# A four-layer decoder trunk on one core: HGRN2's levels in shared series, its outputs turned on VectorE, and norm pieces beside the next layer's work

## The chip, the cores and the metric

The kernel runs on one core of a Trainium2 chip. The metric is the time of one execution in device microseconds (us), shown as the median of three runs. The profile is of one further execution, whose own time is given beside its span.

## The reference

The reference computes four layers over 1024 tokens of width 1024, with mixers HGRN2, sliding-window attention, gated DeltaNet and HGRN2 again. Cut to what the change touches:

```
for i in range(4):
    shift, scale, gate = split(c @ ada_w[i] + ada_b[i])
    h = rmsnorm(x, norm_g[i]) * (1 + scale) + shift
    y = mixer(h)
    x = x + gate * y

# HGRN2, per head of 128, per chunk: b = cumsum(log_f)
A[t, s] = sum_d q[t, d] k[s, d] exp(b[t, d] - b[s, d])        (s <= t)
o = A @ v + (q * exp(b)) @ S
S = exp(b_last) * S + (k * exp(b_last - b)).T @ v
y = (rmsnorm(o, onorm_g) * silu(z)) @ w_out
```

## The kernel before

**Tiling.** x is held transposed (features on partitions) in two halves of 512 tokens, `x[0]` and `x[1]`, 8 blocks of 128x512 each. Every projection is a product of float32 split into a high and a low part (`hi`, `lo`), three matmuls each (`mm3`, lines 201 to 206). `load_w` (166 to 186) brings 128x512 raw weights in over SP's DMA queue into 3 buffers (`RAW`), ScalarE casts the high part (179) and VectorE subtracts for the low part (180), 4 buffers each (`WB`). `proj_fm` (509) runs a 128-column projection for one or both halves, `proj_tm` (1170) one of 256 columns with tokens on partitions.

**Norm.** `norm_stats` (469) makes the row scale and spreads it over partitions into a PSUM bank. `norm_apply` (496) then makes, for each of 8 blocks, `n_t = x * G * rb` on VectorE (504), `hhi = n_t + S` on ScalarE (505) and `hlo` on VectorE (506). `n_t` has 2 SBUF buffers. At a layer's end the main loop (1443 to 1462) runs the norm of the next layer for each half, complete, ahead of the next layer's instructions.

**Order.** The kernel is written as Python generators. `weave` (68) takes from several of them in turn, in proportion to a total given by hand for each; `early` and `tc.high_priority` raise the priority of what is inside. From program order and priority a scheduler makes one fixed order for each engine, and PE, VectorE, ScalarE and SP each run theirs in that order.

**HGRN2** (`hgrn2`, 956). Of each of 8 heads `proj` (969) makes q, f, z and derived tiles, and `mix` (1026) runs beside the next head's projections. For each half, one after the other, `mix` goes through three levels `l` = 1, 3, 5: ScalarE and VectorE fill a tile `X` (1061 to 1063, one buffer), PE makes products of 32-wide blocks into a bank `lev_ps` (16 for level 3, 32 for level 1 at line 1040, 12 for level 5 at line 1087, on 32-column strips of the array), and VectorE picks them into `A` and scales on (1070 to 1098). `tied` (138) puts the products of a series straight behind one another on PE. Then come kh transposes (1104), four chunks of output and state products (1114 to 1124), the norm of the output on VectorE (1132), four PE transposes `ot_ps` (1136), the gate with `zs` (1139) and one 256 KB write to `od` in DRAM (1141). Before the output projection `out_load` (1185) reads `od` back.

**Gated DeltaNet** (`gdn`, 537) starts with the projections of k, q and z of unit 0 for half 0 (920), spills x, runs `decays`, and so on; `conv` (636) is three VectorE steps (650) between ScalarE copies (644, 648) and a tanh (651). Its outputs already go a way without PE: a VectorE multiply in a block order (858), a 32x32 block transpose on VectorE (859) and four 64 KB writes (862). `swa` (1219) starts with k and v of half 0, then of half 1, then q and z of the first group.

```
            r = self.rsqrt(ms, NC, "hg", mp)
            on = tl("tmp")
            nc.vector.tensor_tensor(on..., po..., r..., ALU.mult)
            pt = self.psum("tr", "ot_ps", 1)
            for c in range(NC):
                nc.tensor.transpose(pt[:, cs], on[:, cs], self.ident)
            of = tl("tmp")
            nc.vector.tensor_tensor(of, pt, d["zs", hf], ALU.mult)
            nc.sync.dma_start(od[...], of)
```

## Time and profile before

| | |
|---|---|
| median of 3 runs | 2688.89 us (2688.8 to 2697.25) |
| the profiled execution, its own time | 2695.95 us |
| its span, first to last instruction | 2694.2 us (1.75 us lie around it) |
| PE, VectorE (DVE), ScalarE (ACT) busy | 2609.7, 2010.2, 1272.9 us |
| mean granted TensorE clock | 0.992 |

The layers lie at about 62 to 640 us (HGRN2), 640 to 1118 (attention), 1118 to 2080 (DeltaNet) and 2080 to 2694 (HGRN2). PE's matmuls are pipelined: a record of 0.39 us can start 0.23 us after the one before, so what a group of matmuls costs is read from the distance of starts, not from its record lengths. "Idle" in a row is what the engine waited just before those instructions, and the name behind it is what ended most of that wait.

### The profile page before, as it was taken

The numbers are of one execution on the slowest core, as the hardware profiler recorded it, in microseconds if no ns is written. First come the engines' busy times: TensorE is split into PE (matmuls) and PEld (weight loads), VectorE is DVE, ScalarE is ACT, GpSimd is POOL, SyncE is SP. The second block draws the span as 40 slices with busy tenths as digits, with TensorE's granted clock in tenths as the row PEclk, the third lists the DMA queues.
The fourth block names the chain that finished last, engine by engine and source line by source line (L and its number), as shares of the span: only waits on it lengthen the run. The fifth ranks groups of instructions, "written<-read, shape, count | busy, mean of one in ns | idle before, by whom it ended". The sixth has DMA issues, their size and how long they took to land.

```text
span 2694.2 us, 51458 instructions
## 1 busy us (share of the span) xinstructions
PE 2609.7 (97%) x18927; PEld 2102.4 (78%) x18927; DVE 2010.2 (75%) x5619; ACT 1272.9 (47%) x3268; POOL 136.7 (5%) x352
## 2 busy tenths in 40 slices
PE   8999999999999999999999999999999999999998
PEld 4878878778878777677877777777788878787877
DVE  6776766788687877777988888989876766656575
ACT  4333333444454655454556556666644433333342
POOL 0000100000000000001001101100000000000000
PEclk9999999999999999999999999999999999999999
DMA  6332222344223252333343333333584221111133
GB/s 241 92 93 84 68 79 72 110 137 157 59 87 103 75 158 91 114 98 84 102 115 99 96 105 100 94 97 82 179 254 132 71 60 37 56 51 43 49 118 115
DMA packets 361490, 273.29 MB, mean 101 GB/s; under 512 B 70499, under 2 KB 294166, under 8 KB 361238
## 3 DMA queue, kind: packets, MB, share of 16 engines
q1 hardware_dynamic: 360950, 268.96, 33.9%
q8 instruction: 149, 2.44, 0.4%
q14 instruction: 103, 0.84, 0.1%
q0 software_dynamic: 288, 1.05, 0.1%
HBM read 224.77 MB, written 45.15 MB: 100 GB/s over the span
## 4 chain that ended last, share of the span: by engine, by line
PE 71%; DVE 17%; DMA 5%; ACT 3%; issue 3%; SPq 1%; POOL 0%; DVEq 0%; ACTq 0%; POOLq 0%
PE proj_ps L206 10%; PE proj_ps L205 9%; PE proj_ps L204 9%; PE outp_ps L204 5%; PE outp_ps L205 5%; PE outp_ps L206 5%; DMA ada_w<-in_ada_w_dram 3%; PE projt_ps L204 3%; PE projt_ps L206 3%; PE projt_ps L205 3%; DVE w_lo L180 2%; DVE gd_tb L650 2%; PE pv_ps L1374 1%; DVE ada_acc L413 1%; PE w_ps L890 1%
## 5 line engine op out<-in xcount | busy, mean ns | idle before, releaser
L204 PE MATMUL proj_ps<-hhi,w_hi 128*128 128x512 f32 x1664 | 675.8, 406 | 6.1 <-ACT gd_tb L648 5.9
L206 PE MATMUL proj_ps<-hhi,w_lo 128*128 128x512 f32 x1664 | 679.9, 409 | 0.0
L205 PE MATMUL proj_ps<-hlo,w_hi 128*128 128x512 f32 x1664 | 671.2, 403 | 0.0
L204 PEld LDWEIGHTS proj_ps<-hhi,w_hi 128*128 128x128 f32 x1664 | 315.3, 190 | 59.4 <-ACT gd_tb L648 6.3
L205 PEld LDWEIGHTS proj_ps<-hlo,w_hi 128*128 128x128 f32 x1664 | 314.7, 189 | 59.0 <-issue 2.4
L206 PEld LDWEIGHTS proj_ps<-hhi,w_lo 128*128 128x128 f32 x1664 | 315.0, 189 | 56.1 <-issue 1.0
L179 ACT CAST w_hi<-w_raw 128x512 fp32r<-128x512 f32 x332 | 202.0, 611 | 303.3 <-PE proj_ps L205 188.1
L180 DVE TENSOR_TENSOR w_lo<-w_raw,w_hi 128x512 fp32r<-128x512 f32 x332 | 223.1, 674 | 155.2 <-ACT w_hi L179 129.1
L205 PE MATMUL projt_ps<-w_lo,hhi 128*128 128x256 f32 x896 | 258.7, 291 | 4.7 <-DVE w_lo L180 4.7
L204 PE MATMUL projt_ps<-w_hi,hhi 128*128 128x256 f32 x896 | 257.8, 290 | 0.6 <-ACT w_hi L179 0.6
L206 PE MATMUL projt_ps<-w_hi,hlo 128*128 128x256 f32 x896 | 256.8, 290 | 0.0
L204 PE MATMUL outp_ps<-o_hi,w_hi 128*128 128x512 f32 x576 | 229.2, 400 | 4.7 <-ACT o_hi L1200 3.4
L205 PE MATMUL outp_ps<-o_lo,w_hi 128*128 128x512 f32 x576 | 229.4, 399 | 0.0
L206 PE MATMUL outp_ps<-o_hi,w_lo 128*128 128x512 f32 x576 | 226.8, 396 | 0.7 <-DVE w_lo L183 0.7
L205 PEld LDWEIGHTS projt_ps<-w_lo,hhi 128*128 128x128 f32 x896 | 171.1, 192 | 8.1 <-DVE w_lo L180 6.0
L204 PEld LDWEIGHTS projt_ps<-w_hi,hhi 128*128 128x128 f32 x896 | 171.1, 192 | 3.7 <-ACT w_hi L179 1.0
L206 PEld LDWEIGHTS projt_ps<-w_hi,hlo 128*128 128x128 f32 x896 | 170.8, 192 | 2.4 <-issue 1.0
L650 DVE SCALAR_TENSOR_TENSOR gd_tb<-gd_xs,taps,gd_tb 128x512 f32<-128x512 f32 x192 | 145.2, 756 | 28.3 <-ACT gd_tb L648 19.7
L182 ACT ACTIVATE w_hi<-w_raw,par 128x512 fp32r<-128x512 f32 (+1 forms) x136 | 94.3, 698 | 137.0 <-PE outp_ps L205 89.2
L204 PEld LDWEIGHTS outp_ps<-o_hi,w_hi 128*128 128x128 f32 x576 | 108.8, 189 | 29.1 <-ACT o_hi L1200 4.9
L413 DVE SCALAR_TENSOR_TENSOR ada_acc<-ada_w,par,ada_acc 128x512 f32<-128x512 f32 x140 | 104.8, 749 | 33.4 <-DMA ada_w<-in_ada_w_dram 32.5
L206 PEld LDWEIGHTS outp_ps<-o_hi,w_lo 128*128 128x128 f32 x576 | 108.7, 189 | 23.5 <-DVE w_lo L183 1.3
(398 smaller groups left out, 4894.8 us busy)
## 6 DMA issues: line engine op xcount, KB each, us to landing
ada_w<-in_ada_w_dram SPq DMA_DIRECT2D x160, 256.0 KB, 2.8
w_raw<-in_hg_in_w_dram SPq DMA_DIRECT2D x136, 256.0 KB, 2.8
w_raw<-in_gd_in_w_dram SPq DMA_DIRECT2D x108, 256.0 KB, 3.0
o_in<-od SPq DMA_DIRECT2D x72, 256.0 KB, 3.2
w_raw<-in_gd_out_w_dram SPq DMA_DIRECT2D x64, 256.0 KB, 2.9
w_raw<-in_sw_in_w_dram SPq DMA_DIRECT2D x48, 256.0 KB, 2.9
w_raw<-in_hg_out_w_dram SPq DMA_DIRECT2D x40, 256.0 KB, 2.8
ada_w<-in_ada_w_dram SPq DMA_DIRECT2D x8, 1024.0 KB, 9.2
```

Of the source, the lines that this page charges most:

```text
L179: nc.scalar.copy(hi, raw)
L180: nc.vector.tensor_tensor(lo, raw, hi.bitcast(F32), ALU.subtract)
L182: nc.scalar.activation(hi, raw, AF.Copy, scale=scale)
L204: mm(out, a[0], b[0], start=start, stop=False)
L205: mm(out, a[0], b[1], start=False, stop=False)
L206: mm(out, a[1], b[0], start=False, stop=stop)
L413: self.nc.vector.scalar_tensor_tensor(acc, w, c, acc, ALU.mult, ALU.add)
L650: nc.vector.scalar_tensor_tensor(y, xs[:, j:j + HT], w(j), y, ALU.mult, ALU.add)
L890: nc.tensor.matmul(po[:, hd[a]], dd["u"][a, hf][:, cs], rhs, start=True, stop=True)
L1374: nc.tensor.matmul(po[a * 64:(a + 1) * 64], vg[:, n + 1 - nkb + b, :], p4[:, :, a, :], start=b == 0, stop=b == nkb - 1)
```

## The change

- **HGRN2 levels.** `mix` now takes level l of half 1 together with the next level of half 0: the series of products are (half 0, 1), (half 1, 1 with half 0, 3), (half 1, 3 with half 0, 5) and (half 1, 5). The products of one series are tied. The last head is still done half by half. Level 5 has 16 products instead of 12: the 96 columns of strip 0 become 32 on strip 3 and 64 on strip 0. Buffers change with it.
- **HGRN2 outputs.** For heads 0 to 6 the PE transposes go. VectorE multiplies into block order, transposes 32x32 blocks, four DMAs write to a new DRAM tile `pd`; later `gate` reads `pd` back (256 KB), multiplies by `zs` on VectorE and writes `od`.
- **Norm.** `norm_apply` becomes a generator, `n_t` moves from SBUF to the PSUM banks `lev` (2), and the pieces of half 1 are issued by the next layer: at once in HGRN2 and attention, and in DeltaNet four behind the convolution steps of each of the first two projections. DeltaNet's early part also has z of unit 1 for half 0, and the weave that follows is 10400 shorter.
- **Attention's start.** v and q of half 0 come first, then v of half 1, k of all tokens (its row scales for two blocks at a time), z, and q of half 1.
- **Output.** `x_out` has 3 buffers instead of 5; half 1 uses the 3 raw weight buffers too.

```diff
-NB = {"n_acc": 1, "n_sq": 2, "n_t": 2}
+NB = {"n_acc": 1, "n_sq": 2}
...
+                if hf and c % 2:
+                    xo = self.wp.tile([P, HT], F32, name="x_raw", tag="raw", bufs=RAW)
+                else:
+                    xo = op.tile([P, HT], F32, name="x_out", tag="x_out", bufs=3)
...
         for k in range(KT):
-            t = self.np.tile([P, HT], F32, name="n_t", tag="n_t", bufs=NB["n_t"])
+            t = self.psum("lev", "n_t", 2)
...
+            yield 1
...
             for j in (2, 1, 0):
-                nc.vector.scalar_tensor_tensor(y, xs[:, j:j + HT], w(j), y, ALU.mult, ALU.add)
+                last = nc.vector.scalar_tensor_tensor(y, xs[:, j:j + HT], w(j), y, ALU.mult, ALU.add)
+
+            with self.tc.issue_after(last.ins):
+                drain(take(self.last, self.parts))
...
-        self.early(proj_kq(0, ds[0], ((0,),)), EV)
+        self.parts = 4
+        self.early(chain(proj_kq(0, ds[0], ((0,),)), proj_z(1, ds[1], (0,))), EV)
+        drain(self.last)
...
-              (chain(proj_z(0, ds[0], (1,)), proj_v(0, ds[0]), proj_z(1, ds[1]), proj_kq(1, ds[1])), 72800, 0, 1, 0))
+              (chain(proj_z(0, ds[0], (1,)), proj_v(0, ds[0]), proj_z(1, ds[1], (1,)), proj_kq(1, ds[1])), 62400, 0, 1, 0))
...
-        bufs = {"X": 1, "q": 3, "f": 3, "kg": 3, "qf": 3, "tmp": 3, "v": 3, "zs": 3, "kht": 1, "k0": 2}
+        bufs = {"X": 2, "q": 3, "f": 2, "kg": 4, "qf": 4, "tmp": 3, "v": 3, "zs": 4, "kht": 1, "k0": 2}
...
+        def gate():
+
+            h, hf, z = pend.pop(0)
+            rows = (slice(h * P, (h + 1) * P), slice(hf * HT, (hf + 1) * HT))
+            t = tl("tmp")
+            nc.sync.dma_start(t, self.pd[rows])
+            nc.vector.tensor_tensor(v4(z, "c b"), v4(t, "b c"), v4(z, "c b"), ALU.mult)
+            nc.sync.dma_start(od[rows], z)
...
+                mms = [lambda c=c, m=m: mm(c, *m) for c in range(NC) for m in (
+                    (0, 3, slice(6, 7), slice(3, 4)), (0, 0, slice(0, 4, 3), slice(1, 3)),
+                    (1, 1, slice(1, 5, 3), slice(2, 4)), (2, 2, slice(2, 3), slice(3, 4)))]
...
+            if h < HA:
+
+
+                nc.vector.tensor_tensor(v4(on, "b c"), v4(po, "c b"), r[:, :, None, None].to_broadcast([P, NC, 4, 32]), ALU.mult)
+                ob = tl("tmp")
+                nc.vector.transpose(ob, on)
+                dst = self.pd[h * P:(h + 1) * P, hf * HT:(hf + 1) * HT].rearrange("(b q) (a t) -> a q b t", b=4, a=4)
+                for a in range(4):
+                    nc.sync.dma_start(dst[a], ob[a * 32:(a + 1) * 32].rearrange("q (b t) -> q b t", b=4))
+                pend.append((h, hf, d["zs", hf]))
...
+        def mix(h, d, halves=(0, 1)):
+
+            for hf in halves:
+                level_1(d, hf)
+            steps = [[(halves[0], 1)], [(halves[0], 3)], [(halves[0], 5)], []]
+            for hf in halves[1:]:
+                for n, l in ((1, 1), (2, 3), (3, 5)):
+                    steps[n].append((hf, l))
+            for n, st_ in enumerate(steps):
+                ls = [level(d, hf, l) for hf, l in st_]
+                if ls:
+                    self.tied([m for mms, _ in ls[::-1] for m in mms])
+                    yield 700 + 300 * len(ls)
+                if n == 1 and pend:
+                    gate()
+                for _, rest in ls:
+                    rest()
+                    yield 1
+                if n == 3 and ls:
+                    gate()
+                if n > 1 and n - 2 < len(halves):
+                    yield from outputs(h, d, halves[n - 2])
...
-        self.early(kv(0))
+        self.early(chain(proj_v(0), proj_q(0, ds[0], (0, 1))))
         self.spill_x(1)
-        drain(kv(1))
-        ds = [dict() for _ in range(G)]
-        drain(proj(0, ds[0]))
+        drain(proj_v(1))
+        drain(self.proj_tm(self.load_tm(w_in, 1024), ev_k))
+        drain(chain(proj_z(0, ds[0]), proj_q(0, ds[0], (2, 3))))
...
-                k.norm(nxt, hf)
-                if nxt % 3 and hf == 0:
-                    k.spill_x(0)
-                if hf == 1:
+                a = k.norm_apply(nxt, hf, k.norm_stats(hf))
+                if hf == 0:
+                    drain(a)
+                    if nxt % 3:
+                        k.spill_x(0)
+                else:
+                    k.last = a
                     k.nst.close()
```

## Rows read from the trace of the kernel before

**Rows 1.** The page, part 1: busy time, share of the span, instructions.

```profile
PE 2609.7 (97%) x18927; PEld 2102.4 (78%) x18927; DVE 2010.2 (75%) x5619; ACT 1272.9 (47%) x3268; POOL 136.7 (5%) x352
```

**Rows 2.** PE's waits over the span: engine line waited for: us, times, longest.

```profile
PE lev_ps L1040 <- DVE hg_X L1063: 6.8, 19, 1.8
...
PE proj_ps L204 <- ACT gd_tb L648: 5.9, 1, 5.9
PE ot_ps L1136 <- DVE hg_tmp L1132: 5.6, 11, 1.3
PE projt_ps L205 <- DVE w_lo L180: 4.7, 5, 1.4
...
PE ab_ps L575 <- DVE gd_tb L727: 2.0, 1, 2.0
```

**Rows 3.** Stretches: length, busy us (instructions) of PE, PEld, DVE, ACT, POOL; clock, DMA.

```profile
62.00:520.00 458.00, 446.93 (x4209) 370.84 (x4208) 321.64 (x1012) 162.58 (x388) 28.75 (x60) 1.00 0.28 83
...
1180.00:1260.00 80.00, 77.21 (x534) 62.41 (x535) 63.55 (x161) 40.38 (x109) 8.31 (x20) 0.96 0.39 103
2140.00:2540.00 400.00, 396.14 (x3772) 332.79 (x3771) 247.46 (x848) 143.14 (x345) 25.76 (x56) 1.00 0.16 48
```

**Rows 4.** PE's timeline around one group of output transposes: start, us, line, count.

```profile
365.37 0.39 PE L205 MATMUL proj_ps<-hlo,w_hi 128*128 128x512 f32 x1
365.59 0.60 PE L1136 MATMUL ot_ps<-ident,hg_tmp 128*128 128x128 f32 x4
...
366.26 0.39 PE L204 MATMUL proj_ps<-hhi,w_hi 128*128 128x512 f32 x1
```

**Rows 5.** PE's timeline around series of levels 1, 3 and 5 of one head.

```profile
2225.94 0.55 PE L1040 MATMUL lev_ps<-hg_X,hg_kg 128*32 128x48 f32 x32
2226.31 0.52 PE L1040 MATMUL lev_ps<-hg_q,hg_k 128*32 128x48 f32 x32
...
2228.71 0.39 PE L206 MATMUL proj_ps<-hhi,w_lo 128*128 128x512 f32 x1
2229.07 0.55 PE L1040 MATMUL lev_ps<-hg_X,hg_kg 128*32 128x48 f32 x32
2229.55 0.50 PE L204 MATMUL proj_ps<-hhi,w_hi 128*128 128x512 f32 x1
2229.89 0.39 PE L205 MATMUL proj_ps<-hlo,w_hi 128*128 128x512 f32 x1
...
2232.40 0.39 PE L204 MATMUL proj_ps<-hhi,w_hi 128*128 128x512 f32 x1
2232.72 0.85 PE L1087 MATMUL lev_ps<-hg_X,hg_kg 128*32 128x96 f32 x24
2233.50 0.50 PE L205 MATMUL proj_ps<-hlo,w_hi 128*128 128x512 f32 x1
```

**Rows 6.** VectorE's groups: count, busy us, mean ns, idle before.

```profile
L506 DVE SCALAR_TENSOR_TENSOR hlo<-n_t,mod,hhi 128x512 fp32r<-128x512 f32 x64 | 45.9, 746 | 1.4 <-ACT hhi L505 0.8
...
L859 DVE STREAM_TRANSPOSE gd_of<-gd_of 128x512 f32<-128x512 f32 x32 | 22.5, 704 | 0.1
...
L1198 DVE TENSOR_TENSOR o_z<-o_in,o_z 128x512 f32<-128x512 f32 x32 | 21.8, 687 | 9.6 <-DMA o_z<-zd 6.6 <-issue 1.4 <-DMA o_in<-od 1.2
```

**Rows 7.** ScalarE's groups, 2140 to 2540 us: count, busy us, mean ns, idle before.

```profile
L179 ACT CAST w_hi<-w_raw 128x512 fp32r<-128x512 f32 x58 | 36.1, 622 | 72.0 <-PE proj_ps L205 52.2 <-PE projt_ps L206 11.2 <-DMA w_raw<-in_hg_in_w_dram 7.0
...
L1090 ACT COPY hg_at<-lev_ps 32x384 f32<-32x384 f32 (+2 forms) x42 | 15.2, 363 | 20.3 <-PE lev_ps L1087 19.6
```

**Rows 8.** DMA issues over the span: count, KB each, median us to landing.

```profile
o_in<-od SPq DMA_DIRECT2D x72, 256.0 KB, 3.2
...
od<-gd_of SPq DMA_DIRECT2D x128, 64.0 KB, 1.8
```

**Rows 9.** One stretch at DeltaNet's start, columns as in rows 3.

```profile
1134.50:1141.00 6.50, 3.69 (x9) 2.82 (x9) 5.77 (x10) 4.07 (x8) 2.74 (x9) 0.50 0.33 80
```

**Rows 10.** SP's timeline in DeltaNet: four output writes together, start and us.

```profile
1547.70 1.77 SPq L862 DMA_DIRECT2D od<-gd_of  x4
```

More of the change, by code (lines that the diff above doesn't have):

```diff
@@ L100, in __init__ @@
         self.x = [None, None]
-        self.oo, self.pre = {}, {}
+        self.oo, self.pre, self.last, self.parts = {}, {}, iter(()), 0
     def hslot(self, name):
@@ new lines, in outputs @@
+        def outputs(h, d, hf):
+            kg, qf, v, at, F, S = d["kg", hf], d["qf", hf], d["v", hf], ats[hf], d["F", hf], d.get("S")
+            pt = self.psum("tr", "kh_ps", 1)
+            for c in range(NC):
+                cs = slice(c * P, (c + 1) * P)
+                nc.tensor.transpose(pt[:, cs], kg[:, cs], self.ident)
+            yield 436
+            kht = tl("kht")
+            nc.scalar.copy(kht, pt)
+            po = self.psum("o", "o_ps", 1)
+            ssq = mp.tile([P, NC], F32, name="hg_ssq", tag="hg_ssq", bufs=2)
+            on = tl("tmp")
+            for c in range(NC):
+                cs = slice(c * P, (c + 1) * P)
+                if S is not None:
+                    nc.tensor.matmul(po[:, cs], qf[:, cs], S, start=True, stop=False)
+                nc.tensor.matmul(po[:, cs], at[:, c, :], v[:, c, :], start=S is None, stop=True)
+                yield 436
+                if not (hf == 1 and c == NC - 1):
+                    pS = self.psum("s", "s_ps", 1)
+                    nc.tensor.matmul(pS[:, :P], kht[:, cs], v[:, c, :], start=True, stop=True)
+                    Sn = mp.tile([P, P], F32, name="hg_S", tag="hg_S", bufs=3)
+                    if S is None:
+                        nc.vector.tensor_copy(Sn, pS[:, :P])
+                    else:
+                        nc.vector.scalar_tensor_tensor(Sn, S, F[:, c:c + 1], pS[:, :P], ALU.mult, ALU.add)
+                    S = Sn
+                    yield 218
+                nc.scalar.activation(on[:, cs], po[:, cs], AF.Square, accum_out=ssq[:, c:c + 1])
+            ms = mp.tile([P, NC], F32, name="hg_ms", tag="hg_ms", bufs=2)
+            nc.vector.tensor_scalar(ms, ssq, 1.0 / P, EPS, ALU.mult, ALU.add)
+            r = self.rsqrt(ms, NC, "hg", mp)
+            if h < HA:
[6 more added lines that the diff above has]
+                pend.append((h, hf, d["zs", hf]))
+            else:
@@ L1278, in ev_k @@
[L1278 to L1286 removed]
+            if tp % 2 == 0:
+                ks["ms"] = sp.tile([P, 16], F32, name="k_ms", tag="k_ms", bufs=1)
@@ L1291, in ev_v, with proj_q @@
             nc.scalar.copy(v[:, v2, :], p3)
[L1293 to L1294 removed]
+        def proj_q(g, d, tps=range(4)):
             def ev_q(tp, ps):
@@ L1434, in trunk @@
                 k.preload(hg_in_w[0], (x,))
-        k.norm_apply(layers[0], 0, rb)
-        rb = k.norm_stats(1, k.load_x(sp, 1))
-        k.norm_apply(layers[0], 1, rb)
+        drain(k.norm_apply(layers[0], 0, rb))
+        k.last = k.norm_apply(layers[0], 1, k.norm_stats(1, k.load_x(sp, 1)))
+        drain(k.last)
         if layers[0] % 3:
```

228 lines of the change are left out of this document (96 added, 132 removed).

## The prediction

> **What bounds the kernel now.** I read the busy times first. PE is busy for 97% of the span, VectorE for 75% and ScalarE for 47% [rows 1], so a gain has to come out of PE's own work or out of its waits. PE's waits come second. They are short and scattered, and the reader should note the names: matmuls that wait for VectorE's X tile, one wait of 5.9 us behind a ScalarE convolution copy, eleven in front of the output transposes, five for the low weights [rows 2]. Third come the stretches. In the two HGRN2 layers PE is busy 446.93 of 458 us and 396.14 of 400, VectorE 321.64 and 247.46, ScalarE 162.58 and 143.14 [rows 3], so added VectorE and ScalarE work has cover there. Last comes PE's timeline, where the distance between starts gives a price. Between 2229.89 and 2232.40 us lie eleven steps of ordinary projection matmuls, 0.228 us each [rows 5]; what a foreign group adds is the distance between the projection matmuls around it, less these steps.
>
> The sum below is made against the profiled execution, 2695.95 us; the median is 7.06 us lower, 2688.89, and I subtract the same sum from it. A measurement of this kernel can tell about 0.3%, 8 us, from no change.
>
> **Output transposes.** Four PE transposes go for each of 2 layers x 7 heads x 2 halves, 28 groups. One group stretches the distance of its neighbours from 365.37 to 366.26 us; less two steps of 0.228 it costs 0.43 us [rows 4]. 28 x 0.43 = 12.2 us. The 5.6 us that PE waited ahead of them [rows 2] fall on 32 groups, so 28/32 go, 4.9 us. Together -17.1; it is at least -12.2, if another VectorE step of the chain is waited for instead. What takes their place is off PE: a block transpose on VectorE of 704 ns [rows 6], 28 x 0.70 = 19.7 us over both layers, beside some 290 us in which VectorE is idle in the two stretches [rows 3]; the multiplies before and behind it stay, at the 687 ns that DeltaNet's gate takes in the same block order [rows 6].
>
> **SP's queue** gets four writes instead of one, a read and a write for each group; four such writes take 1.77 us of issue [rows 10]. The final write to `od` stands behind the read's landing (3.2 us for a like read [rows 8]) and a multiply of 0.69: about 3.9 us in which weight loads queue behind it. The cover is that weights are early. The casts that open a weight buffer wait 63.4 us for PE to free one and 7.0 for a DMA [rows 7]. Three raw buffers hold 3 x 24 matmuls x 0.228 = 16 us of PE's work. VectorE's gate waits for its read too: in DeltaNet the same step waits 9.6 us in 32 [rows 6], 0.3 each. I put 28 x 0.15 = +4 us on PE, between 0 and 28 x 0.7 = +20.
>
> **Level 5.** Its products run on strips of 32 columns side by side. A series of level 3 puts 4 x 48 = 192 columns on each strip and takes 0.48 us from its first start to the next projection; level 5 puts 4 x 96 = 384 on the fullest strip and takes 0.78 [rows 5]. So 192 columns cost 0.30. With the fullest strip at 256 it should take 0.48 + 0.10 = 0.58, and 32 series x 0.20 = -6.4 us. The other end is 0: if products and not columns set the pace, 16 instead of 12 give nothing back. I take -6.4, because 16 products of level 3 do run in 0.48. The Trainium skill (TensorEngine Tiling (Array Packing), section Instruction Overhead) says that each matmul has some 60 cycles of overhead on trn2, so that short ones cost as much as 60 columns; by that the rebalanced series would gain nothing, and the sum would be 6.4 us smaller, 2656 for the median, inside the forecast's own range. The trace speaks against it here: 32 records of 48 columns start within 0.37 us, 12 ns apart [rows 5]. ScalarE copies four blocks instead of three, 32 x 0.36 = 12 us more [rows 7], hidden by the 64% of these stretches in which it is idle [rows 3].
>
> **Series in common.** A lone series of level 3 adds 2229.89 - 2228.71 - 2 x 0.228 = 0.72 us to PE. A second sixteen products inside a series adds 0.37 [rows 5]. So each join saves 0.35; 14 heads x 2 joins give -9.8 us. The other end is 0: the cost of entry and exit could come back if products of one series wait for each other. I take -9.8, as the series is tied and the half whose X is made last goes first. The 6.8 us of waits for X [rows 2] I leave as they are: fewer series wait, but each for the later of two tiles. Between -4 and +8 is open.
>
> **Norm beside DeltaNet's start.** Now ScalarE reaches the first convolution copy only behind the norm's pieces, and PE waits 5.9 and then 2.0 us [rows 2]. Across the end of the first wait the clock is at half, 1.2 GHz, for 6.5 us with 3.69 us of PE work [rows 9], which costs 1.85. All of this, 9.7 us, goes if the convolution is issued first and 48 more matmuls of half 0 (z of unit 1, 11 us) stand ready. But they come out of the cover of the inverse that follows, where PE already has 2.8 us idle in 80 and VectorE works 63.6 of 80 [rows 3]. The split projection also loads its weights twice: 4 more loads, casts and subtractions, beside work. I take -8, between -9.7 and +3.
>
> **Attention's start.** PE waits 4.7 us for low weights that VectorE makes too late, between norm pieces and k's evaluation [rows 2]. With v and q first and k later, I take -3; the ends are -4.7 and, as q's evaluation asks as much of VectorE as k's, 0.
>
> **Small parts.** k's row scales for two blocks at once, the PSUM home of `n_t` (same operations, same sizes) and HGRN2's buffer counts cost nothing on PE; each lies beside projections, and a shortage would show as a wait of an evacuation. Fewer `x_out` buffers in the first half: +1, between 0 and +5.
>
> **Sum.** -17.1 + 4 - 6.4 - 9.8 - 8 - 3 + 1 = -39.3 us. That gives 2656.6 for a profiled execution and 2649.6 for the median; 2650.
>
> **Rivals.**
> *The levels wait (2670).* VectorE becomes the pace where two halves' levels come at once. PE's longest wait for X today is 1.8 us [rows 2]; if each of the 28 joined series waits 0.7 us more, 20 us come back. For it: VectorE's 70% is an average over a head. Against: the work is the same, spread over the same head.
> *The norm pieces and the levels get in each other's way (2670).* `n_t` now shares its two PSUM banks with attention's scores at the end of that layer, eight pieces of three 0.75 us steps [rows 6] over two banks, 9 us; and neither start brings anything: 39.3 - 11 - 9 = 19.3. Against: most of that chain has output projections beside it.
> *SP's queue holds up the weights (2700, slower).* At each of the 28 gates the queue stands for 3.9 us behind the read. If the loads behind it are needed at once, PE loses half of that, 28 x 1.95 = 55 us, in place of the 4: -39.3 - 4 + 55 = +11.4. It decides once the weights' lead falls below those 3.9 us; the casts' 7.0 us for DMA against 63.4 for PE [rows 7] speak against it.
> *The change doesn't join the series (2660).* The scheduler could leave them apart; then the 9.8 us stay. Against: they are tied explicitly.
>
> **How the numbers follow.** Forecast 0.56 (own range 2630 to 2662), waiting levels 0.15, norm in the way 0.12, no joins 0.06, SP's queue 0.07, and 0.04 for a gain beyond 2626, all terms at their best ends. The range 2626 to 2676 takes in the unknown bounds and the cases down to the waiting levels, and leaves out SP's queue and some of either tail. Faster by over 0.3% means below 2680.8: the forecast and nearly all of the three weaker cases, 0.87. Within 0.3%, where two of them fall together: 0.06. Slower: 0.07.
>
> **What would show it.** Right: `ot_ps` falls from 32 groups to 4; the level-5 series takes about 0.58 us; four level series a head instead of six, 28 fewer; no wait near 5.9 us at DeltaNet's start and no stretch at 0.50 there; HGRN2's two layers shorter by some 16 us each. Wrong: casts that wait for weight DMAs by more than some 7 us a layer; waits of `lev_ps` for X well over 7 us; new waits of scores for `n_t`; a VectorE above 85% in HGRN2.

## The result, and the profile after

The changed kernel takes 2696.12 us (median of 22 runs, 2690.86 to 2703.11) against 2691.15 for the kernel before (22 runs on the same chips). The ratio is 1.0020, 95% interval 1.0013 to 1.0026: 0.2% slower, within the 0.3% that the forecast called no change. The forecast was 2650, faster by 39.3 us. The profiled execution after took 2696.45 us, its span 2694.8.

The page's part 1 answers to [rows 1]:

```profile
PE 2590.9 (96%) x19071; PEld 2092.7 (78%) x19071; DVE 2025.7 (75%) x5629; ACT 1275.6 (47%) x3304; POOL 135.7 (5%) x352
```

PE's work did shrink, by 18.8 us. The span did not. So PE's idle time grew by as much: span less busy was 84.5 us and is 103.9. PE's waits say where; they answer to [rows 2]:

```profile
PE lev_ps L1079 <- DVE hg_X L1071: 8.5, 17, 2.0
PE proj_ps L207 <- DVE w_lo L181: 6.3, 2, 4.1
PE lev_ps L1079 <- DVE hg_F L1112: 4.4, 10, 0.6
...
PE outp_ps L207 <- DVE w_lo L184: 3.9, 2, 3.2
...
PE lev_ps L1079 <- DVE rs_y L164: 3.7, 2, 2.1
...
PE projt_ps L206 <- DVE w_lo L181: 2.3, 4, 1.2
```

The level series, which waited 6.8 us for X, now wait 8.5 + 4.4 + 3.7 us in the rows shown, though a head has four of them and not six. Two waits of DeltaNet's start, 5.9 us for a convolution and 2.0 for the gates, are gone; two for low weights, 6.3 us, are there. The wait of 3.2 us in the row of `outp_ps` is new too: it stands at the end of layer 0, where the kernel before waits 0.7 for low weights. The 4.7 us at attention's start are 2.3. The 5.6 us ahead of the output transposes are gone with the transposes: one group of 16 is left, 4 for each of four halves.

```profile
L1170 PE MATMUL ot_ps<-ident,hg_tmp 128*128 128x128 f32 x16 | 2.5, 280 | 0.2 <-DVE hg_tmp L1166 0.2
```

The same stretches as in [rows 3], same columns:

```profile
62.00:520.00 458.00, 438.42 (x4193) 367.74 (x4192) 330.10 (x1030) 165.30 (x405) 25.18 (x60) 0.99 0.33 99
1180.00:1260.00 80.00, 76.81 (x367) 62.30 (x366) 66.17 (x174) 43.09 (x117) 2.62 (x12) 1.00 0.38 110
2140.00:2540.00 400.00, 390.37 (x3870) 330.54 (x3869) 260.64 (x868) 144.75 (x362) 28.34 (x56) 1.00 0.21 64
```

VectorE is busy 72% and 65% of the HGRN2 stretches, not over 85%: by the average there is room. One step of a head, between the starts of two joined series, looks otherwise. PE's timeline, then the same 5.6 us as a stretch:

```profile
2338.72 0.54 PE L1079 MATMUL lev_ps<-hg_X,hg_kg 128*32 128x48 f32 x31 [0.37 <-DVE hg_X L1071]
...
2339.88 0.50 PE L206 MATMUL proj_ps<-hlo,w_hi 128*128 128x512 f32 x1
...
2343.46 0.39 PE L206 MATMUL proj_ps<-hlo,w_hi 128*128 128x512 f32 x1
2344.32 0.54 PE L1079 MATMUL lev_ps<-hg_X,hg_kg 128*32 128x48 f32 x31 [0.47 <-DVE hg_F L1112]
```

```profile
2338.70:2344.30 5.60, 5.12 (x112) 4.05 (x113) 5.60 (x25) 1.71 (x4) 1.97 (x4) 1.00 0.16 50
```

VectorE works 5.60 of 5.60 us; PE has sixteen projection products to fill the time (2339.88 to 2343.46), and then waits 0.47. So a wait here is VectorE's time from one series to the next, less what PE was given to do meanwhile. Both can be at fault, and the experiments had to tell which.

In these stretches SP's queue and ScalarE's casts are not it. The casts wait 7.8 us for weight DMAs in the last stretch, 7.0 before [rows 7], and the gates wait 14.4 us in 28, 0.5 each, where 0.3 had been taken from DeltaNet:

```profile
L180 ACT CAST w_hi<-w_raw 128x512 fp32r<-128x512 f32 x58 | 36.1, 622 | 64.0 <-PE proj_ps L206 50.1 <-DMA w_raw<-in_hg_in_w_dram 7.8 <-PE projt_ps L207 4.2
```

VectorE's groups over the span, as in [rows 6]:

```profile
L1160 DVE STREAM_TRANSPOSE hg_tmp<-hg_tmp 128x512 f32<-128x512 f32 x28 | 19.8, 706 | 0.3
L1044 DVE TENSOR_TENSOR hg_zs<-hg_tmp,hg_zs 128x512 f32<-128x512 f32 x28 | 19.3, 689 | 14.4 <-DMA hg_tmp<-pd 14.1
```

### The profile page after: what moved, and what is told of

It is laid out like the page before. It is cut to its first block, busy times and chain, and to the rows that moved or that the text cites. A ratio compares the mean times of both kernels' runs of the same rounds, so it can differ in the third digit from the quotient of the medians.

```text
span 2694.8 us, 51993 instructions
## 1 busy us (share of the span) xinstructions
PE 2590.9 (96%) x19071; PEld 2092.7 (78%) x19071; DVE 2025.7 (75%) x5629; ACT 1275.6 (47%) x3304; POOL 135.7 (5%) x352
## 4 chain that ended last, share of the span: by engine, by line
PE 40%; DVE 11%; DMA 2%; issue 1%; ACT 1%; SPq 1%; POOL 0%; DVEq 0%; ACTq 0%
PE proj_ps L207 6%; PE proj_ps L206 6%; PE proj_ps L205 6%; PE outp_ps L206 3%; PE outp_ps L205 3%; PE outp_ps L207 3%; DVE gd_tb L654 1%; PE w_ps L897 1%; PE w_ps L913 1%; PE S_ps L902 1%; PE ks_ps L886 1%; PE ks_ps L887 1%; DVE w_lo L181 1%; PE projt_ps L206 1%; PE projt_ps L207 1%
## 5 line engine op out<-in xcount | busy, mean ns | idle before, releaser
L654 DVE SCALAR_TENSOR_TENSOR gd_tb<-gd_xs,taps,gd_tb 128x512 f32<-128x512 f32 x192 | 144.5, 753 | 16.7 <-ACT gd_tb L652 14.4
```

The costliest lines, as they stand in the source:

```text
L654: last = nc.vector.scalar_tensor_tensor(y, xs[:, j:j + HT], w(j), y, ALU.mult, ALU.add)
```

## The experiments

Each kernel was timed beside the kernel before on the same chip, so times are compared by their ratios to it: a difference of 0.001 is 2.7 us. The intervals are 0.0007 to 0.0015 to either side, so a difference of two ratios is uncertain by some 4 us, and by 5 to 6 between the widest. All runs:

| kernel | median us | ratio to before (95%) |
|---|---|---|
| changed kernel | 2696.12 | 1.0020 (1.0013 to 1.0026) |
| e1_split | 2698.83 | 1.0024 (1.0011 to 1.0038) |
| e2_halves | 2698.42 | 1.0024 (1.0013 to 1.0036) |
| e3_norm | 2685.68 | 0.9976 (0.9968 to 0.9985) |
| e4_pe_out | 2697.09 | 1.0013 (1.0005 to 1.0022) |
| e6_relief | 2688.76 | 0.9998 (0.9989 to 1.0007) |
| e7_l5 | 2692.35 | 1.0004 (0.9995 to 1.0012) |
| e8_nomask | 2699.69 | 1.0031 (1.0020 to 1.0042) |
| e9_swa | 2694.67 | 1.0013 (1.0004 to 1.0022) |
| f1_pace | 2673.35 | 0.9933 (0.9918 to 0.9947) |
| f2_pace13 | 2676.77 | 0.9943 (0.9931 to 0.9955) |
| g1_pace | 2694.81 | 1.0014 (1.0006 to 1.0023) |
| g2_pace_l5 | 2693.18 | 1.0003 (0.9993 to 1.0013) |
| h1_pace_split | 2676.70 | 0.9943 (0.9930 to 0.9956) |
| h2_pace_pe_out | 2688.83 | 0.9980 (0.9969 to 0.9990) |
| h3_pieces_only | 2688.18 | 0.9982 (0.9973 to 0.9991) |
| h5_pace_out | 2671.75 | 0.9925 (0.9912 to 0.9939) |
| h6_pace_l5old | 2681.46 | 0.9962 (0.9947 to 0.9977) |
| h7_change_pace | 2686.58 | 0.9977 (0.9966 to 0.9988) |

### First: one part taken back at a time

**e1_split**, the joins taken apart:

```
-                    self.tied([m for mms, _ in ls[::-1] for m in mms])
-                    yield 700 + 300 * len(ls)
+                    for mms, _ in ls:
+                        self.tied(mms)
+                        yield 700
```

> The changed kernel, only that the two halves' levels of a step go in two series, each tied by itself, instead of one in common; 28 series more, everything else as it is. Theory A (the joins save TensorE 0.35 us each, and that saving stands in the changed kernel's time): 28 x 0.35 = 9.8 us slower than the changed kernel, about 2706 us, ratio to the kernel before near 1.0055. Theory B (the joined series stand at VectorE's pace, each waits for the later of two tiles, and the waits take back what the joins save): TensorE's work 9.8 us longer, but its waits for VectorE in the levels some 8 us shorter, time within 3 us of the changed kernel's 2696.

1.0024 against 1.0020: the joins bring 1 us. Theory B by the time, and the three longest rows of the level series' waits sum to 11.0 us for 16.6. PE's busy time did not grow, though (2590.8 us for 2590.9); these profiled executions differ in clock (0.992 for 0.991), which hides a part.

**e2_halves**, no interleaving of the halves:

```
+            for hf in halves:
+                for l in (1, 3, 5):
+                    mms, rest = level(d, hf, l)
+                    self.tied(mms)
...
+                yield from outputs(h, d, hf)
```

> The changed kernel with a head's first half through all three levels and its outputs before the second half begins, as before the change; outputs by VectorE, the rebalanced level 5 and the norm's pieces stay. Theory A (interleaving the halves is what fills VectorE's pace, so that it helps): six lone series a head again, 9.8 us of TensorE's work back, waits as they are, about 2706. Theory B (the interleaving itself makes the waits, 19 us of lev_ps waits against 7): work 9.8 us longer and waits 12 us shorter, about 2694 or a little faster than the kernel before (2691). Theory C (VectorE's transposes and gates make the waits, not the interleaving): waits stay near 19 us and the time is 2706 or more.

Also 1.0024. In time the interleaving neither makes the loss nor saves anything. But PE's waits show that two things cancel: in place of 8.5 + 4.4 + 3.7 us, X has this one row of size, near the kernel before.

```profile
PE lev_ps L1079 <- DVE hg_X L1071: 7.6, 19, 1.1
```

So the waits come with the interleaved, joined series, as theory B had it, and theory C is out; but with the halves apart PE's own work is longer again (busy 2601.8 us for 2590.9), so that B's gain in time did not come.

**e4_pe_out**, the outputs transposed by PE again:

```
-            if h < HA:
...
-                nc.vector.transpose(ob, on)
...
+            if True:
...
                 pt = self.psum("tr", "ot_ps", 1)
...
+                if h < HA:
+                    nc.sync.dma_start(od[h * P:(h + 1) * P, hf * HT:(hf + 1) * HT], of)
```

> The changed kernel with the outputs of heads 0 to 6 transposed by TensorE and written once, as before the change; joined series, level 5 and norm stay. Theory A (taking the transposes from TensorE is worth its 12.2 us and more): 12 to 17 us slower than the changed kernel, 2708 to 2713. Theory B (VectorE sets the pace of the levels, and its 20 us of block transposes come back as waits for X, F and S): TensorE's work 12 us longer, its waits in the HGRN2 layers 8 to 12 us shorter, time within 4 us of 2696.

1.0013, if anything 2 us faster than with VectorE's transposes. Theory B by the time: the part that carried 13.1 us of the forecast brings nothing here. PE's busy time is 9.3 us longer (2600.2) and its span 1.1, because the waits for X and F halve, as theory B asked:

```profile
PE lev_ps L1079 <- DVE hg_F L1112: 5.4, 12, 0.6
PE lev_ps L1079 <- DVE hg_X L1071: 2.9, 10, 0.7
```

This run alone can't say why: VectorE is 14.3 us lighter (2011.4 busy), and PE has the transposes to do between two series.

**e3_norm**, the norm's pieces at once and DeltaNet's old start:

```
-                    k.last = a
+                    drain(a)
...
-        self.early(chain(proj_kq(0, ds[0], ((0,),)), proj_z(1, ds[1], (0,))), EV)
+        self.early(proj_kq(0, ds[0], ((0,),)), EV)
...
-              (chain(proj_z(0, ds[0], (1,)), proj_v(0, ds[0]), proj_z(1, ds[1], (1,)), proj_kq(1, ds[1])), 62400, 0, 1, 0))
+              (chain(proj_z(0, ds[0], (1,)), proj_v(0, ds[0]), proj_z(1, ds[1]), proj_kq(1, ds[1])), 72800, 0, 1, 0))
```

> The changed kernel with the norm's pieces of the second half issued at once, and DeltaNet's start as before the change (only keys and queries of unit 0 ahead of the rest). Theory A (the new start saves what I forecast): 8 us slower than the changed kernel, 2704. Theory B (the 5.9 and 2.0 us of waits only changed their names: TensorE now waits 2.1 + 4.1 us for low weights at the same place): within 2 us of 2696, with one wait near 6 us for a convolution copy and none of 4 us for low weights at DeltaNet's start. Theory C (late pieces cost elsewhere, such as the 3.2 us wait for low weights at the end of layer 0): 3 us or more faster.

0.9976: 11.8 us under the changed kernel. Theory C by its sign, though at another place than it named: the 3.2 us wait at the end of layer 0 is still there. Changed kernel, DeltaNet's start, VectorE:

```profile
1133.19 0.69 DVE L659 SCALAR_TENSOR_TENSOR gd_k<-gd_tb 128x512 f32<-128x512 f32 x1 [2.20 <-ACT gd_tb L658]
...
1146.66 0.69 DVE L734 SCALAR_TENSOR_TENSOR gd_tb<-gd_tb,proj_ps 128x512 f32<-128x512 f32 x1 [0.95 <-ACT gd_tb L733]
1147.26 1.40 DVE L509 SCALAR_TENSOR_TENSOR hlo<-n_t,mod,hhi 128x512 fp32r<-128x512 f32 x2
1148.58 1.88 DVE L181 TENSOR_TENSOR w_lo<-w_raw,w_hi 128x512 fp32r<-128x512 f32 x3
```

and what PE does meanwhile, then two stretches of the changed kernel and one of e3_norm (columns as in [rows 3]; the third from the end is the clock):

```profile
1149.32 0.80 PE L207 MATMUL proj_ps<-hhi,w_lo 128*128 128x512 f32 x1 [4.13 <-DVE w_lo L181]
```

```profile
1138.50:1141.90 3.40, 3.36 (x9) 2.16 (x8) 3.40 (x7) 1.28 (x3) 0.18 (x1) 0.50 0.29 74
...
1148.80:1152.20 3.40, 2.88 (x7) 2.33 (x8) 1.67 (x3) 0.00 (x0) 0.00 (x0) 0.50 0.52 148
```

```profile
1120.00:1160.00 40.00, 38.79 (x176) 29.11 (x175) 34.36 (x71) 22.90 (x55) 2.72 (x11) 1.00 0.37 104
```

Tied behind the convolutions, VectorE's queue comes to stand where a convolution waits for ScalarE (2.20 us, then 0.95), the norm's pieces slip behind it, and the low weights behind the pieces: three of them are made together from 1148.58, and when PE goes on at 1149.32 it has stood for 4.13 us. Two stretches at half clock, 1.2 GHz, lie behind the first wait and across the end of the second. In e3_norm 38.79 of 40 us are work, at full clock. The old wait of 5.9 us did not come back with the old start. ScalarE's first copy of a convolution, in the kernel before and in e3_norm:

```profile
1136.10 0.57 ACT L644 COPY gd_xs<-proj_ps 128x512 f32<-128x512 f32 x1
...
1120.12 0.59 ACT L648 COPY gd_xs<-proj_ps 128x512 f32<-128x512 f32 x1 [2.27 <-PE proj_ps L207]
```

Before, it stands behind the norm's eight pieces on ScalarE; in e3_norm it comes ahead of them, 1.4 us behind the start of half 1's norm sums on PE (1118.7) and not 18.3. So e3_norm has at this place what the forecast wanted, without pieces tied behind convolutions. Of the change's norm only `n_t` in PSUM is left there; that it turned the order was not tried alone.

### Second: does VectorE set the pace?

**e6_relief** (on e3_norm) moves two VectorE steps of layer 3 to ScalarE; **e8_nomask** (on e3_norm) leaves seven masked copies a half out, so that its scores lack levels 1 and 3.

```
-                    nc.vector.tensor_scalar(f, f, om, lb, ALU.mult, ALU.add)
-                    nc.vector.tensor_scalar(k0, k0, om, None, ALU.mult)
+                    nc.scalar.activation(f, f, AF.Identity, bias=lb, scale=om)
+                    nc.scalar.activation(k0, k0, AF.Copy, scale=om)
```

```
-                    nc.vector.copy_predicated(av, self.lmask[0, 1].rearrange("p (c n) b j -> p c (n b j)", c=NC), pv[:, :, 32:])
...
-                    for n, b0 in ((1, 0), (2, 3), (3, 5)):
-                        nc.vector.copy_predicated(av[:, :, n:, :], self.lmask[l, n], pv[:, :, b0:b0 + 4 - n, :])
```

> The kernel of e3_norm, with the two scalings of the forget gate's tiles (f and k0, 0.54 and 0.48 us on VectorE, 16 of each, only in layer 3 whose lower bound isn't zero) done by ScalarE; TensorE's work is untouched, VectorE loses 16 us beside the levels of one layer. Theory A (VectorE, busy without a gap while levels run, sets when each series can start): the waits for X and F in layer 3 fall from 8 us to 5 or less, time 3 to 5 us under e3_norm's 2685.7, near 2682. Theory B (a layer's average counts, VectorE has 35% to spare and the waits are the latency of a chain): no change, 2684 to 2688.

> The kernel of e3_norm without the masked copies that put the products of levels 1 and 3 into the score tile (seven VectorE steps a half, some 0.9 us; 32 halves, 30 us in all); the scores then hold only their diagonal and level 5. TensorE's instructions are the same. Theory A (VectorE sets the pace of the levels): waits of the level series fall from 19 us to under 10, time 8 to 12 us under e3_norm's 2685.7, 2674 to 2678. Theory B (VectorE's average has room): the 30 us were hidden, 2684 to 2688.

In time both fell out against both theories. With 28 us less on VectorE (1996.2 busy for 2024.3) and the same PE instructions, e8_nomask is 14.8 us *slower* than e3_norm (1.0031 against 0.9976); e6_relief is 5.9 us slower. That one tells little: the waits of `lev_ps` in layer 3 did fall, from 7.3 us to 5.3, while layer 0, whose instructions are untouched, took 4.0 us longer in its profiled execution, with 23.9 us at half clock for 6.8. PE's waits of e8_nomask, and one step of a head, on PE's timeline:

```profile
PE lev_ps L1079 <- DVE hg_X L1071: 14.5, 22, 2.0
PE lev_ps L1079 <- DVE hg_F L1109: 6.1, 8, 0.9
```

```profile
2341.06 0.54 PE L1079 MATMUL lev_ps<-hg_X,hg_kg 128*32 128x48 f32 x31 [0.92 <-DVE hg_X L1071]
...
2344.85 0.54 PE L1079 MATMUL lev_ps<-hg_X,hg_kg 128*32 128x48 f32 x31 [0.76 <-DVE hg_X L1071]
```

With VectorE's chain shorter, the next series starts 3.79 us after the last and not 5.60. But the scheduler had put only 7 projection products between the two, where it has 16 in e3_norm and in the changed kernel (counted on the timeline of a head of layer 3), so PE waits longer, 0.76 us for 0.47. The two rows are 7.5 us over e3_norm's 8.1 + 5.0, half of the 14.8; the granted clock gives at most 2 us more (21.6 us for 19.5 by the formula of the last section, means of 8 and 11 runs), and the rest was not traced. That gave a third theory, C: **the fixed order of PE is what loses the time.** On this reading the scheduler puts a series where, by its own reckoning, X is just ready, and what VectorE really takes beyond that is a wait, once for each series, whatever VectorE's load.

### Third: the order alone

**f1_pace** (on e3_norm) leaves every instruction as it is, and lets a level series go only behind the projection product that was written last ahead of it, with the head's steps spread over all projections beside them:

```
+                with self.tc.issue_after(behind.ins):
+                    first = mms[0]()
...
-        mm(out, a[1], b[0], start=False, stop=stop)
+        self.pm = mm(out, a[1], b[0], start=False, stop=stop)
...
-                    self.tied([m for mms, _ in ls[::-1] for m in mms])
+                    self.tied([m for mms, _ in ls[::-1] for m in mms], self.pm)
...
-            weave(self.tc, (mix(h, ds[h]), 16000, 0, 1, PRH), (g, 41600, 0, 1, 0), (take(side, ns), ns, 0, 1, 0))
+            weave(self.tc, (mix(h, ds[h]), 10600, 0, 1, PRH), (g, 41600, 0, 1, 0), (take(side, ns), ns, 0, 1, 0))
```

> The kernel of e3_norm; each level series may be issued only behind the projection product that was written last ahead of it, and the levels and outputs of a head are spread over all of the projections beside them (10600 in place of 16000 in the interleaving). Same instructions, another order: 18 to 24 projection products stand between a head's first three series where e3_norm has 10 to 27. Theory C (a wait is the time of VectorE's chain between two series less the projections that the planner put between them; whoever makes VectorE lighter makes it put fewer): the 19 us of waits for X and F fall under 8, 10 us under e3_norm, 2676. Theory A (VectorE sets the pace of a head whatever the order): waits move to other products (outputs, states), time within 3 us of 2685.7.

0.9933, 11.6 us under e3_norm and 18 under the kernel before. The waits that were 8.1 + 5.0 + 3.3 us in e3_norm are one row:

```profile
PE o_ps L1143 <- ACT hg_at L1114: 7.2, 12, 1.1
...
PE outp_ps L209 <- ACT o_hi L1259: 4.7, 3, 2.6
...
PE lev_ps L1083 <- DVE hg_X L1075: 2.5, 3, 0.9
```

Theory C's number and its waits both came. What is late next stands in the same rows: outputs that wait for ScalarE's copies of the scores.

**f2_pace13**, the same with 13000:

> As f1_pace with 13000 in place of 10600: 18, 18 and then 5 projection products between the series, so less room ahead of the second series. Theory C: between e3_norm and f1_pace, waits of 8 to 14 us, near 2680. Theory A: as e3_norm, 2684 to 2688.

0.9943, 2.7 us over f1_pace, within the uncertainty. Here theory C's number failed: the waits for X are 0.5 us and not 8 to 14. Eighteen projection products between two series already cover VectorE's chain here; the sixteen and seven above didn't.

**g1_pace** is the same pacing put into the kernel before, **g2_pace_l5** adds the new level 5 to it:

```
+                        self.tied([lambda c=c, m=m: mm5(c, *m) for c in range(NC) for m in xk], self.pm)
...
-            weave(self.tc, (mix(h, ds[h]), 16000, 0, 1, PRH), (g, 41600, 0, 1, 0), (take(side, ns), ns, 0, 1, 0))
+            weave(self.tc, (mix(h, ds[h]), 11400, 0, 1, PRH), (g, 41600, 0, 1, 0), (take(side, ns), ns, 0, 1, 0))
```

> The kernel before, with its level series (each tied, each half by itself, level 5 as it was) issued only behind the projection product written last ahead of them, and spread over the projections (11400): 12 projection products between series where it had 4 to 20. Theory C: its 8 us of waits for X fall by half, 3 to 4 us faster than before, 2687. Theory A: no change, 2690 to 2692.

> g1_pace with the rebalanced products of level 5; the order of the two is nearly the same, so that this pair prices level 5 without a new order. Theory C (level 5's 6.4 us are real on TensorE and were lost in e7_l5 to another order and its waits): 5 to 7 us faster than g1_pace. Rival (the saving isn't there, since the chain of a head sets the time): within 2 us of g1_pace.

g1_pace is 3.8 us *slower* than the kernel before: with only 7 us of such waits there was little to win, and the output projections at the ends of the layers, with the heads' steps now later, wait 10.6 us (4.2, 2.9, 2.4 and 1.1) for 4.9. Its clock is lower too: by the formula of the last section g1_pace loses 25.0 us at half clock (mean of 11 runs) and the kernel before 17.9 (23 runs), more than the whole difference. So the pacing is no gain of its own; it gives back what the joined series had lost. Level 5 takes 3.0 us off it, inside the uncertainty and half of the term.

### Fourth: the terms of the sum, priced where the order leaves room

**e7_l5**: level 5 alone, put into the kernel before (sixteen tied products, four copies, as in the change).

> The kernel before with the rebalanced products of level 5 alone (sixteen tied products instead of twelve, four ScalarE copies instead of three). Theory A (TensorE's saving stands): 32 x 0.20 = 6.4 us faster than before, 2685, ratio 0.9976. Theory B (what TensorE saves between VectorE's steps comes back as waits, as it did with the joins and with the output transposes): 0 to 2 us faster, ratio above 0.999.

1.0004: nothing. PE is busy 9.5 us less (2600.2), but four waits that the kernel before doesn't have, up to 2.1 us each, take most of it back: a head's first output now comes before GpSimd's copy of the diagonal blocks has ended.

```profile
PE o_ps L1116 <- POOL hg_at L1081: 6.7, 4, 2.1
```

**h6_pace_l5old**, **h1_pace_split** and **h2_pace_pe_out** each take one part back out of f1_pace: level 5's old products, the joins, VectorE's transposes (the edits of e1_split and e4_pe_out, and level 5's lines of before).

> f1_pace with level 5's products as before the change (twelve instead of sixteen, the fullest strip with 384 columns instead of 256, three ScalarE copies instead of four). Theory C (32 series x 0.20 us of TensorE's work, not eaten where the order leaves room): 6.4 us slower than f1_pace's 2673.4, 2680. Rival (the fourth copy and the scores' wait for it take the saving back, as in e7_l5): within 2 us of f1_pace.

> f1_pace with the two halves' series of a step apart, each behind the projection written last ahead of it; 28 series more. Theory C (the joins' 0.35 us each are real and were eaten by waits for the later of two tiles): with the waits paced away, 28 x 0.35 = 9.8 us slower than f1_pace's 2673.4, 2683. Rival (a join saves nothing, TensorE's cost at a series' ends comes back in the joined one): within 2 us of f1_pace.

> f1_pace with the outputs of heads 0 to 6 transposed by TensorE, as before the change. Theory C (the 12.2 us of TensorE's work are real, and the waits of 5 us for the scaled output too): 12 to 17 us slower than f1_pace, 2685 to 2690. Rival (they were hidden behind a bound that stays, as in e4_pe_out, which lost 1 us): within 4 us of f1_pace.

Against f1_pace's 0.9933: level 5 is worth 7.8 us (0.9962), VectorE's transposes 12.6 (0.9980), the joins 2.7 (0.9943). The first two are what theory C asked for. The joins aren't, though PE's own price was right. Part of f1_pace's timeline, a joined series of levels 3 and 1 between projections:

```profile
2325.76 0.39 PE L211 MATMUL proj_ps<-hhi,w_lo 128*128 128x512 f32 x1
2326.08 0.55 PE L1083 MATMUL lev_ps<-hg_X,hg_kg 128*32 128x48 f32 x32
...
2327.58 0.39 PE L210 MATMUL proj_ps<-hlo,w_hi 128*128 128x512 f32 x1
```

and the same two series apart, in h1_pace_split:

```profile
2320.32 0.39 PE L211 MATMUL proj_ps<-hhi,w_lo 128*128 128x512 f32 x1
2320.63 0.55 PE L1083 MATMUL lev_ps<-hg_X,hg_kg 128*32 128x48 f32 x32
...
2321.79 0.40 PE L210 MATMUL proj_ps<-hlo,w_hi 128*128 128x512 f32 x1
...
2325.43 0.39 PE L211 MATMUL proj_ps<-hhi,w_lo 128*128 128x512 f32 x1
2325.75 0.55 PE L1083 MATMUL lev_ps<-hg_X,hg_kg 128*32 128x48 f32 x32
...
2326.57 0.40 PE L210 MATMUL proj_ps<-hlo,w_hi 128*128 128x512 f32 x1
```

Less two steps of 0.228 each, the joined one adds 1.36 us, the two apart 1.01 + 0.68 = 1.70: 0.33 saved, where 0.35 was forecast. If all 28 are like this one, 28 x 0.33 = 9.3 us of PE's work, of which the time shows 2.7, with an uncertainty of some 4 to 5. PE's busy time is 6.5 us longer in h1_pace_split and its span 1.3, so the rest is in waits. f1_pace's row of 7.2 us, outputs that wait for ScalarE's copies of the scores, is nearly gone with the series apart, and its 2.5 us for X are gone altogether:

```profile
PE o_ps L1143 <- ACT hg_at L1114: 0.5, 2, 0.3
```

So with the joins PE loses 9.2 us in these two rows, about what it saves.

**h5_pace_out** (on f1_pace) holds the key transposes and the outputs back in the same way:

```
+            yield 600
+            with self.tc.issue_after(self.pm.ins):
+                for c in range(NC):
...
+                    nc.tensor.transpose(pt[:, cs], kg[:, cs], self.ident)
```

> f1_pace with the transposes of the keys and the first output products held back in the same way, behind the projection written last ahead of them, with 600 more in the interleaving between the last level and the outputs (11800 in all). Theory C: the 12 us of waits of o_ps for the copied scores and the 2 us of kh_ps go to under 5 us, 2665 to 2669. Rival (the head's chain then ends too late, and the end of the layer waits for it): within 3 us of 2673, with more waits of outp_ps.

0.9925, the fastest, though not told apart from f1_pace. The waits for the scores' copies went, and the rival's came: the last head ends later, and the output projections behind it wait.

```profile
PE outp_ps L209 <- ACT o_hi L1262: 18.4, 3, 9.5
```

### Fifth: the starts of the layers

**h3_pieces_only** is the changed kernel with `drain(a)` for `k.last = a` alone; **h7_change_pace** is the changed kernel with f1_pace's pacing; **e9_swa** is e3_norm with the old `swa`.

> The changed kernel with the norm's pieces issued at once, as in e3_norm, but with the early projection of unit 1 kept. Theory P (the pieces, put behind VectorE's convolution steps, hold up the low weights): as e3_norm, 2684 to 2688. Theory Z (the early projection, whose weights come twice, is what costs): as the changed kernel, 2694 to 2698.

> The changed kernel, norm's pieces and DeltaNet's start included, with the level series paced as in f1_pace. If the two causes are independent: 12 us under the changed kernel's 2696 and 10 us over f1_pace, 2684. If DeltaNet's start costs only in company of the old order: near f1_pace, 2676 or less.

> The kernel of e3_norm with attention's start and key evaluation as before the change (keys, then values, then queries). My forecast gave the new start 3 us, so 2688.7; the rival gives it nothing, as the wait for low weights went from 4.7 to 2.3 us while layer 1 as a whole got only 0.8 us shorter in the profile: 2684 to 2687. If the new order hurts, it is under 2684.

h3_pieces_only is 10.2 us under the changed kernel (0.9982), so the pieces and not the early projection cost the time. h7_change_pace is 11.6 us under the changed kernel and 11.8 over f1_pace (0.9977): the tied pieces and the order are two independent losses, of 10 to 12 us each. In e9_swa the old start of attention costs 10.0 us, three times the term; its waits for low weights are 5.5 us for 2.1 in e3_norm, so most of the 10.0 is in no row shown:

```profile
PE projt_ps L206 <- DVE w_lo L181: 5.5, 4, 2.9
```

This prices the start inside a kernel that has the rest of the change. Against the kernel before, which has the same old order, the account is another one, below.

## Why the prediction was wrong

The forecast had the mechanism of PE's work right in nearly every term, and was wrong in what the sum left at rest. First, where the time is. A layer is taken here from the start of half 1's norm sums on PE (`n_ps`) to the next layer's; one profiled execution each, so that a few us say nothing by themselves:

| layer | before, us | forecast | changed kernel | e3_norm | f1_pace |
|---|---|---|---|---|---|
| HGRN2, layer 0 | 638.9 | (both layers) -29.3 | +0.4 | -3.6 | -12.0 |
| attention | 478.9 | -3 | +4.6 | +4.5 | +4.0 |
| DeltaNet | 1005.0 | -8 | -1.2 | -8.9 | -9.4 |
| HGRN2, layer 3, to the end | 571.4 | | -3.2 | -4.4 | -7.2 |

Three steps failed.

**"The 6.8 us of waits for X [rows 2] I leave as they are."** They rose to over 16. The forecast priced each edit by PE's distances, as if what stands between two series would stay enough to cover VectorE. But the same fixed order that made the old waits small was made anew, and a step now holds two halves of VectorE's work and one series of PE's. f1_pace shows the cause: the same instructions in another order are 11.6 us faster, with the waits at 2.5. The rival "the levels wait" had this kind, with 20 us for 28 joined series where the rows shown rose by 10, but gave VectorE's load as the cause. That e8_nomask, with 28 us less on VectorE, is slower speaks against load: what counts is the projections that PE is given between two series. The bound of +8 on this step was too near as well. In the two HGRN2 layers PE is busy 21 us less and idle 18 us more, 10 of them in these rows; the layers were to be 16 us shorter each and changed by +0.4 and -3.2.

**"I take -8, between -9.7 and +3"**, the norm beside DeltaNet's start. The layer is 1.2 us shorter, next to nothing; with the pieces at once it is 8.9 shorter (e3_norm), and the kernel 10 to 12 us faster (h3_pieces_only, e3_norm). So the gain was there to be had, and the tied pieces lost it again. The step counted the wait that goes and named no queue behind the moved pieces. They are issued on VectorE behind a convolution that waits for ScalarE, and three low weights stand behind them. The 5.9 us became 2.1 + 4.1 under another name, with half clock behind each as before [rows 9]. Of the sign "no wait near 5.9 us at DeltaNet's start and no stretch at 0.50 there" the first half is met and the second is not: the wait changed its name, and the two stretches at 0.50 gave it away.

**"With v and q first and k later, I take -3."** The layer is 4.6 us longer; it takes 480 to 488 us in the fifteen kernels here with this order and 477 to 479 in the four that have the kernel before's layer. Its first part did gain 3.3 us: from 638.9 to 1047.84 in the kernel before, from 639.3 to 1044.93 in the changed one. What lost is the last part, from half 0's norm sums to half 1's, 77.9 us for 70.0. Before, then after:

```profile
1047.84 0.95 PE L486 MATMUL n_ps<-ones,n_acc 128*128 128x1 f32 x8
...
1117.83 1.05 PE L486 MATMUL n_ps<-ones,n_acc 128*128 128x1 f32 x8 [0.43 <-DVE n_acc L483]
```

```profile
1044.93 0.95 PE L488 MATMUL n_ps<-ones,n_acc 128*128 128x1 f32 x8
...
1122.78 0.95 PE L488 MATMUL n_ps<-ones,n_acc 128*128 128x1 f32 x8
```

All sixteen kernels here with `n_t` in PSUM take 75.2 to 78.4 us there, the four with it in SBUF (the kernel before, e7_l5, g1_pace, g2_pace_l5) 70.0 to 70.9. The sum took that move as a small part that costs nothing. `n_t`'s old home alone was not tried, so the cause stays open. The wait for low weights at the end of layer 0 goes the same way: it is in all sixteen, 3.2 to 3.7 us, and in the other four 0.7, or 2.4 to 2.6 where the series are paced.

The terms one by one: the forecast, what the changed kernel shows, and what f1_pace shows, where the order leaves room:

| step | forecast | in the changed kernel | in f1_pace |
|---|---|---|---|
| output transposes with SP's queue | -17.1 + 4 | +1.9 (e4_pe_out) | -12.6 (h2_pace_pe_out) |
| level 5 | -6.4 | not tried | -7.8 (h6_pace_l5old) |
| joins | -9.8 | -1.1 (e1_split) | -2.7 (h1_pace_split) |
| DeltaNet's start | -8 | -1.2 (its layer); +10 to +12 against pieces at once | +11.8 against pieces at once (h7_change_pace) |
| attention's start | -3 | +4.6 (its layer) | +4.0 (its layer) |

The parts of f1_pace add up to more than the 18 us by which it is faster (24.6 in its profiled execution): -12.6, -7.8, -2.7 and DeltaNet's 9 make 32. Attention's layer takes 4 of that back; for the rest no run here has a price.

*Output transposes.* The size was right, and its lower bound was wrong. "At least -12.2" took PE's work that goes for time that goes; the changed kernel shows that all of it can come back as waits. The queue behind the gates was right: 0.5 us for a gate, and no later weights in the stretches shown.

*Level 5.* The series came out as forecast: in the paced kernel it adds 0.57 us, from 2300.67 to 2301.24, where 0.58 was said.

```profile
2300.67 0.65 PE L1094 MATMUL lev_ps<-hg_X,hg_kg 128*32 128x32 f32 x32
2301.24 0.50 PE L209 MATMUL proj_ps<-hhi,w_hi 128*128 128x512 f32 x1
```

The Trainium skill (TensorEngine Tiling (Array Packing), section Instruction Overhead) puts some 60 cycles on each matmul; if they added up product after product, as the prediction read it, sixteen short products would cost more than twelve. These sixteen take 0.57 us for 0.78 [rows 5], and h6_pace_l5old is 7.8 us slower, so on strips side by side they do not add up here. But alone, in the kernel before, most of the term was lost to waits for GpSimd's copy (e7_l5), which the step did not name.

*Joins.* 0.33 us a join for PE, as forecast. The time has 1 to 3 of the 9.3 us. The step that failed is the one that let PE's saving count in full; in the paced kernel the rest is in the outputs' waits for copied scores and in the last 2.5 us for X.

*Norm pieces and levels.* That rival named the end of attention and 9 us, and 7.9 us are lost there. But the waits that it described are not seen: `n_t` waits 8.6 us over its 64 steps, 8.4 of them for its inputs, and scores wait 0.9 us for a piece. Place and size came, the mechanism is not shown. Its other half, that the starts bring nothing, was right for DeltaNet for another reason, and wrong for attention's first part.

*Other rivals.* SP's queue held up no weights in the stretches shown (7.8 us of ScalarE's waits for DMA, as before), and the joins are made. Fewer `x_out` buffers were not tried alone.

*Range.* Its upper end, 2676, took in "the cases down to the waiting levels", each alone. Here waiting levels, a start without gain and a longer end of attention came together. The prediction gave 0.06 to two of its cases falling together, though nothing ties one to the other.

## What to carry to other kernels

Price PE's saved work by distances, but do not book it as time before asking what PE will do in the freed place: between two steps of a chain on another engine, work that went from PE without other work put there came back as a wait. Where a scheduler fixes the order, a lighter engine can make the kernel slower, so after such a change the order is tuned first (here 11.6 us, by holding a series back behind projections), and the parts are judged after that. A step that is tied behind an instruction is costed by everything that stands behind it in that engine's queue while that instruction waits. And a term is measured against the kernel that it was forecast for: what a part loses inside the changed kernel is not what it loses against the kernel before, and a table by layer shows the difference.

The best version here is the change with the norm's pieces at once and the level series paced: 0.9933 of the kernel before (f1_pace), 0.9925 with the outputs paced too (h5_pace_out).

## What the runs showed of the hardware

Stretches at half clock stand beside some of PE's short waits and add to what they cost. The granted clock of a whole run gives a bound on the time lost at half clock, (1 - clock) x span, which would be lost if PE worked all through these stretches: a mean of 18.5 us over 35 runs of the kernel before, 21.9 over 22 of the changed kernel, 25.2 over 12 of e1_split. In the changed kernel the 4.13 us wait at 1149 and the 2.14 us one at 1137 lie beside stretches at 0.50, shown above; e3_norm, without them, has 1.00 from 1120 to 1160. So of the 5 us by which the changed kernel is slower, up to 3.4 are clock, and even with the clock set aside the change saved nothing.
